# Token tiles of every fourth group of 32 tokens, and the gates' exchange moved around the rotary query products

## The chip, the cores and the metric

The kernel runs on one core of a Trainium2 chip. TensorE (PE) multiplies matrices into PSUM, ScalarE (ACT) and VectorE (DVE) work on PSUM and SBUF, GpSimd (POOL) and SyncE (SP) issue DMAs; the transfers of both queues run on the core's 16 DMA engines. The metric is the device time of one execution in microseconds, the median of several runs.

## The reference, cut to what matters

Two layers over 512 tokens of width 2048. Each layer normalises the tokens, projects them to 4928 columns, runs three groups of heads on the parts, gates the joined result, projects it back and adds it to the tokens:

```python
for l in range(DEPTH):                                  # 2
    z = rmsnorm(x, pre_norm_g[l]) @ w_in[l]             # (512, 2048) @ (2048, 4928)
    q_lat, kv_lat, k_pe, gb, gc, xin, q_mem, gate = split_cols(z)
    # group A: 8 heads; q and k carry 64 rotary columns beside 128 plain ones
    a_out = mla_attention(q, k, v)                      # softmax over all 512 positions, (512, 1024)
    # group B: width-3 convolution along the positions
    c_out = gb * conv3(gc * xin, conv_w[l])             # (512, 512)
    # group C: 4 heads over 256 memory tokens
    m_out = memory_attention(q_mem, rmsnorm(mem), ...)  # (512, 512)
    y = concatenate([a_out, c_out, m_out]) * silu(gate) # (512, 2048)
    x = x + rmsnorm(y @ w_o[l], post_norm_g[l])
```

The convolution is the one place where neighbouring positions meet; everything else treats a token alone or sums over all of them.

## The kernel before, in words

Tokens lie in four tiles of 128. Tile t holds the tokens 128 t to 128 t + 127, one to a partition, so a tensor "by tokens" is a slab [128 partitions, 4 tiles, 512 columns]. The two large projections (`group`, line 488) are done as a block scheme with seven products P1 to P7 in place of eight; every operand is split into two parts (`split_to`, line 275: ACT writes the rounded part, DVE the rest), and each product is three matmuls (`mm3`, lines 271 to 273).

A layer runs the input projection in five column groups, then the `mixer` (line 1248: four memory heads, then eight attention heads, with the query, key and value products of the next pair of heads between them), then the output projection (`out_proj`, line 1289).

Heads work "by features": y is kept as four slabs of [128 features, 4 blocks, 512 tokens]. The gate comes out of the projection by tokens and has to be turned. ACT applies SiLU (line 781), DVE turns every 32x32 block in place (`blocks_turned`, line 918, put off with `pr.defer` at the end of `gated`), and 16 DMAs on SP's queue put the blocks at their places (`exchange`, lines 922 to 929; a run is 32 numbers of 4 bytes). `gate_rows` (line 931) first calls `pr.until`, which issues put-off work until all four tiles are turned, then the 16 DMAs. This is done for three slabs in each layer: `gm` (beside the memory queries) during the last column group, `ga1` after the first plain query product of the mixer, `ga0` three steps further. The head's result is multiplied with the gate in place (line 1199). The convolution (`conv_turn`, line 937) transposes on PE, takes its three taps on DVE straight from PSUM, and multiplies with the transposed gb.

The rotary part of the queries (`q_rope_steps`, line 1034) is two products for four heads, and `rotate0`: four DVE products with the tables, a split, two DMAs away and, later, four DMAs back, all on POOL's queue.

After the heads, y is cut into quarters (`y_blocks`, line 1284; tokens 0 to 255 and 256 to 511) and split for the output projection. The last stage (`fin` and `residual`, lines 1325 and 1374) squares and sums the result, scales it, adds the old tokens (line 1382), and in the last layer sends each tile to the output from SP's queue, a row of the output from a partition (line 1384): two halves of 512 KB for each of the tiles 0 to 2, and five pieces for tile 3, 128, 128, 256, 256 and 256 KB.

Order: PE, SP and POOL issue in the order in which the program is written; ACT and DVE are ordered by a planner with a model of costs. Work given to `pr.defer` has a price and is issued where the steps' `room` allows it, or when `until` asks for it. Weights are loaded some eight units ahead through eight buffers, "raw", which the rotary tables and products share. SP takes its DMAs strictly in order, and the exchange stands between the weight loads.

```python
def exchange(dst, src):
    for p in range(4):
        for b in range(4):
            a = src[32 * p:32 * p + 32].rearrange("i t c k -> i (c t) k")[:, :, 32 * b:32 * b + 32]
            y = dst[32 * b:32 * b + 32].rearrange("i c (t k) -> i (c t) k", k=P)[:, :, 32 * p:32 * p + 32]
            nc.sync.dma_start(y, a)
```

Of the kernel before, what the change touches and what calls it, by code (L numbers as in the profile page):

```python
# [58 lines left out]
PI_DOWN = 3.1415925  # L59

RAW, PIECES, SLABS = 8, 4, 19


class Unit:
# [20 lines left out]
class Program:  # L85
# [23 lines left out]
    def add(self, fn, units=(), room=0.0, ahead=None):  # L109

        self.steps.append((list(units), fn, room, self.ahead if ahead is None else ahead))
# [115 lines left out]
def encoder(tc, x, xt, mem, memt, positions, columns, w_in, q_norm_g, w_uq, w_qr, kv_norm_g, w_ukv,  # L227
# [32 lines left out]
    def slab(name, dt=F32):  # L260
        return slabs.tile([P, D], dt, tag="slab", name=nm(name))

    def scrap(name, w=512, dt=F32):
        return piece.tile([P, 512], dt, tag="piece", name=nm(name))[:, :w]
# [135 lines left out]
    class Left:  # L400
# [1 line left out]

        def __init__(self, by_tokens):
            self.by_tokens = by_tokens
            self.ops = {}

        def split(self, name, p, src):
            t = self.ops[name, p] = slab(f"{name}{p}", F32R)  # L410
            c = src.shape[-1]
            split_to(t[:, :1024].rearrange("p (k c) -> p k c", c=c), t[:, 1024:].rearrange("p (k c) -> p k c", c=c), src)

# [3 lines left out]
        def stationary(self, name, kt, tt):  # L417
            if self.by_tokens:
                t, o = self.ops[name, tt], kt * P
            else:  # L420
                t, o = self.ops[name, kt // 4], (kt % 4) * 256 + tt * P
            return t[:, o:o + P], t[:, 1024 + o:1024 + o + P]

    def combine(left, p, a11, a12, a21, a22):
# [63 lines left out]
    def group(left, key, w, block, slot, passes, final, hold=None, by_two=False, direct=None):  # L488
# [51 lines left out]
        def ended(q, tt):  # L540
            ps = bk[q][tt][:, :w]
            s = {(i, j): slot(i, j, tt) for i in range(2) for j in range(2)}
            if len(s[0, 0].shape) == 3:
                ps = ps.rearrange("p (c k) -> p c k", c=4)
            if q == "P1":
                if keep:
                    nc.scalar.copy(s[1, 0], ps)
                    plus(s[0, 0], s[0, 0], ps)
                    final(0, 0, tt)
                elif apart:  # L550
                    nc.scalar.copy(s[1, 0], ps)
                elif passes is STEADY:
                    nc.scalar.copy(s[0, 0], ps)
                else:
                    plus(s[0, 0], s[0, 0], ps)
                    final(0, 0, tt)
            elif q == "P2":
                if shared:
                    nc.scalar.copy(s[0, 0], ps)
                else:  # L560
                    plus(s[0, 0], s[1, 0] if apart else s[0, 0], ps)
                    final(0, 0, tt)
            elif q == "P5":
                if apart:
                    plus(s[1, 1], s[1, 0], ps)
                else:
                    nc.scalar.copy(s[1, 0], ps)
            elif q == "P6":
                if apart:
                    plus(s[1, 1], s[1, 1], ps)  # L570
                else:
                    plus(s[0, 1], s[1, 0], ps)
            elif q == "P3":
                nc.vector.tensor_tensor(s[0, 1], ps, s[1, 1] if apart else s[0, 1], op=ALU.subtract)
                final(0, 1, tt)
            elif q == "P7":
                if apart:
                    nc.vector.scalar_tensor_tensor(s[1, 1], ps, -1.0, s[1, 1], op0=ALU.mult, op1=ALU.subtract)
                    plus(s[1, 0], s[1, 0], ps)
                else:  # L580
                    nc.scalar.copy(s[1, 1], ps)  # L581
                    nc.vector.scalar_tensor_tensor(s[1, 1], s[1, 1], -1.0, s[1, 0], op0=ALU.mult, op1=ALU.subtract)
                final(1, 1, tt)
            elif direct:
                direct(1, 0, tt, ps)
            else:
                if apart:
                    plus(s[1, 0], s[1, 0], ps)
                else:
                    nc.scalar.copy(s[1, 0], ps)  # L590
                final(1, 0, tt)
# [143 lines left out]
    def projection(l):  # L735
# [8 lines left out]
        def own(*names):  # L744
            def f():
                for n in names:
                    C[n] = slab(n).rearrange("p (c t k) -> p t c k", c=4, t=NT)
            return f

        def slot_of(a, b):  # L750
# [154 lines left out]
    def turn4(view, j, dst=None):  # L905

        ps = bank("tps")
        for t in range(NT):
            v = view(t)
            nc.tensor.transpose(ps[:, t * P:(t + 1) * P], v[:, j] if len(v.shape) == 3 else v[:, j * P:(j + 1) * P], G["ident"])  # L910
        return ps

    def y_slab(k):
        if k not in G["ys"]:
            G["ys"][k] = slab("y").rearrange("p (j c) -> p j c", j=4)
        return G["ys"][k]

    def blocks_turned(v):

# [2 lines left out]
    def exchange(dst, src):  # L922


        for p in range(4):
            for b in range(4):
                a = src[32 * p:32 * p + 32].rearrange("i t c k -> i (c t) k")[:, :, 32 * b:32 * b + 32]
                y = dst[32 * b:32 * b + 32].rearrange("i c (t k) -> i (c t) k", k=P)[:, :, 32 * p:32 * p + 32]
                nc.sync.dma_start(y, a)

    def gate_rows(k, name, C):
        def f():
# [3 lines left out]

    def conv_turn(l, c, C):
        def f():
            u = turn4(lambda t: C["gc"][:, t], c)
            y, w = y_slab(2)[:, c, :], G[f"cw{l}"]  # L940
            nc.vector.tensor_scalar_mul(y, u, w[:, 1, c:c + 1])
            nc.vector.scalar_tensor_tensor(y[:, 1:], u[:, :S - 1], w[:, 0, c:c + 1], y[:, 1:], op0=ALU.mult, op1=ALU.add)
            nc.vector.scalar_tensor_tensor(y[:, :S - 1], u[:, 1:], w[:, 2, c:c + 1], y[:, :S - 1],
                                           op0=ALU.mult, op1=ALU.add)
            g = turn4(lambda t: C["gb"][:, t], c)
            nc.vector.tensor_tensor(y, y, g, op=ALU.mult)
        return f

    def qm_turn(j, C):
# [187 lines left out]
    def head_iters(j, rope, src, keys, whole=False):  # L1137
# [50 lines left out]
        def av(b):  # L1188
            def g():
                if b == 0 or whole:  # L1190
                    st["o"] = bank("o")
                VH, VL = src()[1]
                o = st["o"] if whole else st["o"][:, b * 256:(b + 1) * 256]
                PT = st.pop("PT" if whole else ("PT", b))
                for k in range(kts):
                    mm3(o, (VH(k), VL(k)), (PT[0][:, k], PT[1][:, k]), k == 0, k == kts - 1)
                if b == 1:
                    y = G["ys"][j // 4][:, j % 4, :]
                    nc.vector.tensor_tensor(y, st["o"], y, op=ALU.mult)
            return g  # L1200
        return [((score(t), [], 0.4), trans(t), av(t // 2) if t == 3 or t == 1 and not whole else None, 4 if whole and kts > 2 else 5)
                for t in range(NT)]
# [45 lines left out]
    def mixer(l, C, pair2, tail):  # L1248
# [1 line left out]
        add(tables_fetch)  # L1250
        add(mem_fetch)
        (p0, rotate0, fetch0), (p1, rotate1, fetch1) = (q_rope_steps(l, g) for g in range(2))
        put(p0, rotate0)
        sts = [{} for _ in range(4)]
        qkv = qkv_steps(l, 0, sts[0])
        qkv[0] += (0.0, 1)
        qkv[2] += (0.0, 0)
        put(qkv[:1])
        add(gate_rows(1, "ga1", C))
        its = [it for i in range(4) for it in mem_head(i)]  # L1260
        m = len(its)
        between = {k: [s] for k, s in zip((2, 5, 8, 10, 12), qkv[1:])}
        between.setdefault(3, []).append((gate_rows(0, "ga0", C), []))
        between.setdefault(6, []).append((fetch0, []))
        between[m - 2] = [(lambda: pr.prep_next(), [])]
        for pair in range(4):
# [14 lines left out]
        pipeline(its, between, m)  # L1281


    def y_blocks(p):
        ys = G["ys"]
        a, b = ys[p], ys[2 + p]
        return a[:, :, :256], b[:, :, :256], a[:, :, 256:], b[:, :, 256:]

    def out_proj(l):
        last = l == depth - 1  # L1290
# [83 lines left out]
    def residual(l, st, t):  # L1374
# [4 lines left out]
        def part(c, n=1024):  # L1379
            cs = slice(c, c + n)  # L1380
            xt = st["x"][t]
            nc.vector.scalar_tensor_tensor(xt[:, cs], og[:, cs], st["r", t], xt[:, cs], op0=ALU.mult, op1=ALU.add)
            if last:
                nc.sync.dma_start(out[0][rows, cs], xt[:, cs])
            else:
                nc.gpsimd.dma_start(G["dst"][rows, cs], xt[:, cs])

# [35 lines left out]
    def put(*passes):  # L1423
        for steps in passes:
            for s in steps:
                add(*s)
# [20 lines left out]
    for l in range(depth):  # L1447
# [129 lines left out]
        lat = [latent_turn(l, "cq", j) for j in range(4)] + [latent_turn(l, "ckv", j) for j in range(2)] + [k_rope_turn]  # L1577
        more = [(f, []) for f in lat + [qm_turn(j, C) for j in range(4)]]
        put(weave(g4[16:], more, 2, 2))
        G["left"] = Y = Left(False)  # L1580
        g0, g1, gains, fetch = out_proj(l)

        def low(p):
            return lambda: G["left"].split("A12", p, G["ys"][2 + p][:, :, :256])

        def use_y(Y=Y):
            G["left"] = Y

        def sums(p):
            def f():  # L1590
                a, b = G["ys"][p], G["ys"][2 + p]
                left = G["left"]
                pr.defer(1.2, lambda: left.split("A11", p, a[:, :, :256]))
                pr.defer(1.2, lambda: left.split("A22", p, b[:, :, 256:]))
                combine(left, p, a[:, :, :256], b[:, :, :256], a[:, :, 256:], b[:, :, 256:])
            return f

        last_pair = {0: [(sums(0), []), g0[0][0]], 1: [g0[0][1]], 2: [g0[0][2]], 3: [g0[0][3]],
# [61 lines left out]
```

## Time and profile before

| | |
|---|---|
| median of three runs | 1475.88 us (1475.15 to 1478.01) |
| profiled execution: its own time | 1475.58 us |
| profiled execution: span, first to last instruction | 1473.8 us |
| TensorE busy | 1454.6 us |
| VectorE busy | 1102.1 us |
| ScalarE busy | 862.1 us |
| GpSimd busy | 269.9 us |
| mean granted TensorE clock | 0.998 |
| DMA packets in all | 193344, of them 60576 under 512 B |
| bytes moved | 295.21 MB |

The span is what the trace shows; the execution's own time is 1.8 us longer. Busy time says what an engine did, not what it held up; the tables of waits and the chain of work say that. "SPq" and "POOLq" are the queues that issue DMAs. "To landing" is the time from a DMA's issue until its data is there. A DMA share of 1.00 means that the packets of the transfers filled all 16 DMA engines.

### The profile page before, as it was taken

The page shows a single profiled execution, that of the slowest core. Times are in us where ns is not written, and L with a number is a line of the kernel's source. Part 1 is how long each engine was busy: PE and PEld are TensorE (multiplying, and loading weights), DVE is VectorE, ACT ScalarE, POOL GpSimd, SP SyncE. Part 2 cuts the span into 40 slices and gives each one's busy share as a digit, 9 for nine tenths or more (in the row PEclk, how much of TensorE's full clock was granted, in tenths as well). Part 3 has the DMA queues.
Part 4 walks back from the last instruction along what each step waited for, and adds up shares of the span by engine and source line. Part 5 has one row for each costly group of instructions (what it writes and reads, how often), then busy time and mean ns, then how long its engine had stood idle before and what let it go on. Part 6 is the DMA issues. An engine that isn't in the chain of part 4 may idle for free.

```text
span 1473.8 us, 19452 instructions
## 1 busy us (share of the span) xinstructions
PE 1454.6 (99%) x7104; PEld 1239.6 (84%) x7104; DVE 1102.1 (75%) x1469; ACT 862.1 (58%) x1312; POOL 269.9 (18%) x276
## 2 busy tenths in 40 slices
PE   9999999999999999999999999999999999999997
PEld 8887888899887888888898888888988878888886
DVE  5899677857577778868779666776576777788687
ACT  7856344446458788654777434444464686786443
POOL 0032302031301010321210333030322000004111
PEclk9999999999999999999999999999999999999999
DMA  9999978698989292695987999796979784128945
GB/s 358 403 274 219 219 188 179 166 195 221 207 232 165 75 275 91 124 231 154 339 289 227 235 232 223 195 170 173 210 199 214 230 157 104 40 86 153 266 110 186
DMA packets 193344, 295.21 MB, mean 200 GB/s; under 512 B 60576, under 2 KB 83616, under 8 KB 189408
## 3 DMA queue, kind: packets, MB, share of 16 engines
q0 software_dynamic: 56576, 129.51, 43.7%
q1 hardware_dynamic: 136672, 164.45, 36.3%
q8 instruction: 56, 0.92, 0.3%
q14 instruction: 40, 0.33, 0.1%
HBM read 266.01 MB, written 21.63 MB: 195 GB/s over the span
## 4 chain that ended last, share of the span: by engine, by line
PE 95%; DMA 2%; DVE 1%; ACT 1%; issue 0%; SPq 0%; POOLq 0%; DVEq 0%; ACTq 0%
PE P L272 23%; PE P L273 23%; PE P L271 23%; PE ptp L1184 2%; PE o L272 1%; PE o L273 1%; PE sc L273 1%; PE sc L271 1%; PE sc L272 1%; PE o L271 1%; PE tps L910 1%; PE sc L1165 1%; PE qps L272 1%; PE qps L271 1%; PE qps L273 1%; PE sc L1166 1%
## 5 line engine op out<-in xcount | busy, mean ns | idle before, releaser
L188 ACT CAST wh<-wr 128x1024 fp32r<-128x1024 f32 (+2 forms) x436 | 444.5, 1023 | 448.2 <-PE P L273 340.1
L189 DVE TENSOR_TENSOR wl<-wr,wh 128x1024 fp32r<-128x1024 f32 (+2 forms) x436 | 515.7, 1187 | 251.1 <-ACT wh L188 247.7
L271 PE MATMUL P<-wh,S 128*128 128x512 f32 (+1 forms) x896 | 345.3, 385 | 0.0
L273 PE MATMUL P<-wh,S 128*128 128x512 f32 (+1 forms) x896 | 343.9, 384 | 0.0
L272 PE MATMUL P<-wl,S 128*128 128x512 f32 (+1 forms) x896 | 343.9, 384 | 0.0
L272 PE MATMUL P<-wl,A 128*128 128x512 f32 (+1 forms) x656 | 252.2, 384 | 1.4 <-DVE wl L189 1.4
L271 PE MATMUL P<-wh,A 128*128 128x512 f32 (+1 forms) x656 | 253.1, 386 | 0.0
L273 PE MATMUL P<-wh,A 128*128 128x512 f32 (+1 forms) x656 | 251.9, 384 | 0.0
L145 POOL DMA_DIRECT2D wr<-in_w_in_dram x132 | 158.3, 1199 | 445.3 <-DVE wl L189 261.8
L273 PEld LDWEIGHTS P<-wh,S 128*128 128x128 f32 x896 | 168.3, 188 | 30.1
L272 PEld LDWEIGHTS P<-wl,S 128*128 128x128 f32 x896 | 168.4, 188 | 29.6
L271 PEld LDWEIGHTS P<-wh,S 128*128 128x128 f32 x896 | 168.3, 188 | 29.4
L272 PEld LDWEIGHTS P<-wl,A 128*128 128x128 f32 x656 | 123.3, 188 | 24.4 <-DVE wl L189 2.8
L273 PEld LDWEIGHTS P<-wh,A 128*128 128x128 f32 x656 | 123.2, 188 | 22.1
L271 PEld LDWEIGHTS P<-wh,A 128*128 128x128 f32 x656 | 123.2, 188 | 21.6 <-ACT og L581 0.2
L145 POOL DMA_DIRECT2D wr<-in_w_o_dram x40 | 48.4, 1248 | 297.8 <-DVE wl L189 294.1
L1171 ACT ACTIVATE P<-sc,nm 128x512 f32<-128x512 f32 (+1 forms) x96 | 59.2, 617 | 30.3 <-DVE nm L1168 29.7
L1168 DVE TENSOR_REDUCE nm<-sc 128x1 f32<-128x512 f32 (+1 forms) x96 | 56.9, 596 | 13.3 <-PE sc L273 7.1
L1174 ACT ACTIVATE P<-P,rec 128x512 f32<-128x512 f32 (+1 forms) x96 | 60.6, 652 | 6.6 <-DVE rec L1173 6.6
L1184 PE MATMUL ptp<-identr,P 128*128 128x128 f32 x320 | 46.5, 274 | 2.3 <-ACT P L1174 2.3
L1184 PEld LDWEIGHTS ptp<-identr,P 128*128 128x128 f32 x320 | 37.9, 141 | 9.5 <-ACT P L1174 2.7
L177 DVE TENSOR_TENSOR wr<-wr,wr 128x1024 f32<-128x1024 f32 (+1 forms) x36 | 42.2, 1175 | 3.6 <-DMA wr<-in_w_in_dram 3.2
(317 smaller groups left out, 2070.1 us busy)
## 6 DMA issues: line engine op xcount, KB each, us to landing
wr<-in_w_in_dram SPq DMA_DIRECT2D x128, 512.0 KB, 5.4
wr<-in_w_in_dram POOLq DMA_DIRECT2D x108, 512.0 KB, 7.6
wr<-in_w_o_dram SPq DMA_DIRECT2D x48, 512.0 KB, 6.4
wr<-in_w_o_dram POOLq DMA_DIRECT2D x40, 512.0 KB, 6.9
wr<-in_w_in_dram SPq DMA_DIRECT2D x32, 416.0 KB, 3.8
wr<-in_w_in_dram POOLq DMA_DIRECT2D x24, 416.0 KB, 6.0
wr<-in_w_mk_dram SPq DMA_DIRECT2D x15, 512.0 KB, 8.6
wr<-in_w_mv_dram SPq DMA_DIRECT2D x15, 512.0 KB, 10.5
```

The costliest lines, as they stand in the source:

```text
L145: engine.dma_start(dst, src, **kw)
L177: nc.vector.tensor_tensor(tiles[a], tiles[a], tiles[b], op=ALU.add)
L188: pin(nc.scalar.copy(hi[:, h], src[:, h]))
L189: pin(nc.vector.tensor_tensor(lo[:, h], src[:, h], hi[:, h].bitcast(F32), op=ALU.subtract))
L271: nc.tensor.matmul(ps, ah, bh, start=first, stop=False, **kw)
L272: nc.tensor.matmul(ps, ah, bl, start=False, stop=False, **kw)
L273: nc.tensor.matmul(ps, al, bh, start=False, stop=last, **kw)
L910: nc.tensor.transpose(ps[:, t * P:(t + 1) * P], v[:, j] if len(v.shape) == 3 else v[:, j * P:(j + 1) * P], G["ident"])
L1168: nc.vector.tensor_reduce(nmax, ps, axis=AX.X, op=ALU.max, negate=True)
L1171: nc.scalar.activation(pt, ps, AF.Exp, bias=nmax, accum_out=tot)
L1174: nc.scalar.activation(pt, pt, AF.Copy, scale=rec)
L1184: nc.tensor.transpose(ps[:, k * P:(k + 1) * P], pt[:, k * P:(k + 1) * P], G["ident"])
```

## The change

A tile now holds every fourth group of 32 tokens: partition 32 p + j of tile t is token 128 p + 32 t + j. The host hands over x and the positions in that order. The three gate slabs are laid out with the four tiles' blocks side by side, (group of 32 columns, tile, 32 columns), so that a run of the exchange is 128 numbers, 512 bytes, and y has its tokens in their natural order. What comes from PE by tiles (a transposed tensor, a head's result) is read through `of_tiles`, and y is read and written through `in_tiles`, both with runs of 32 numbers. The convolution needs neighbours, so ACT copies the transposed u to SBUF in natural order, ACT makes the middle tap, and DVE's two other taps read SBUF. The quarters of y for the output projection are taken with `y_half`, runs of 64 numbers, and `split` writes them in runs of 32 (`apart`). The output is written through a view that puts the tokens back: its first dimension is the four p, its second the 32 j. In the mixer, the exchange of `ga1` is issued ahead of the rotary products p0, the exchange of `ga0` between p0 and `rotate0`.

```diff
+BLOCKS = "gm", "ga0", "ga1"
         def split(self, name, p, src):
             t = self.ops[name, p] = slab(f"{name}{p}", F32R)
+            if self.apart:
+                hi, lo = (t[:, o:o + 1024].rearrange("p (t g j) -> p g t j", t=2, j=32) for o in (0, 1024))
+                split_to(hi, lo, src.rearrange("p g (t j) -> p g t j", j=32))
+                return
...
-                    C[n] = slab(n).rearrange("p (c t k) -> p t c k", c=4, t=NT)
+                    C[n] = slab(n).rearrange("p (g t j) -> p t g j" if n in BLOCKS else "p (t g j) -> p t g j", t=NT, j=32)
...
+    def of_tiles(a):
+        return a.rearrange("q (t p j) -> q t p j", t=NT, j=32)
+    def in_tiles(a):
+        return a.rearrange("q (p t j) -> q t p j", t=NT, j=32)
...
         for p in range(4):
             for b in range(4):
-                a = src[32 * p:32 * p + 32].rearrange("i t c k -> i (c t) k")[:, :, 32 * b:32 * b + 32]
-                y = dst[32 * b:32 * b + 32].rearrange("i c (t k) -> i (c t) k", k=P)[:, :, 32 * p:32 * p + 32]
-                nc.sync.dma_start(y, a)
+                a = src[32 * p:32 * p + 32].rearrange("i t (c b) j -> i c b (t j)", b=4)[:, :, b]
+                nc.sync.dma_start(dst[32 * b:32 * b + 32, :, P * p:P * p + P], a)
...
-            u = turn4(lambda t: C["gc"][:, t], c)
+            ps = turn4(lambda t: C["gc"][:, t], c)
             y, w = y_slab(2)[:, c, :], G[f"cw{l}"]
-            nc.vector.tensor_scalar_mul(y, u, w[:, 1, c:c + 1])
+            u = scrap("u")
+            nc.scalar.copy(in_tiles(u), of_tiles(ps))
+            nc.scalar.activation(y, u, AF.Copy, scale=w[:, 1, c:c + 1])
...
-            nc.vector.tensor_tensor(y, y, g, op=ALU.mult)
+            nc.vector.tensor_tensor(in_tiles(y), in_tiles(y), of_tiles(g), op=ALU.mult)
...
-                    nc.vector.tensor_tensor(y, st["o"], y, op=ALU.mult)
+                    nc.vector.tensor_tensor(in_tiles(y), of_tiles(st["o"]), in_tiles(y), op=ALU.mult)
...
-        put(p0, rotate0)
+        add(gate_rows(1, "ga1", C))
+        put(p0)
+        add(gate_rows(0, "ga0", C))
+        put(rotate0)
...
         put(qkv[:1])
-        add(gate_rows(1, "ga1", C))
...
-        between.setdefault(3, []).append((gate_rows(0, "ga0", C), []))
...
-    def y_blocks(p):
-        ys = G["ys"]
-        a, b = ys[p], ys[2 + p]
-        return a[:, :, :256], b[:, :, :256], a[:, :, 256:], b[:, :, 256:]
+    def y_half(k, h):
+        return G["ys"][k].rearrange("q c (p k) -> q (c p) k", k=P)[:, :, 64 * h:64 * h + 64]
...
             if last:
-                nc.sync.dma_start(out[0][rows, cs], xt[:, cs])
+                nc.sync.dma_start(out[0].rearrange("(p t j) c -> t p j c", t=NT, j=32)[t][:, :, cs], xt[:, cs])
...
+    def tiles(a):
+        return a.reshape(1, 4, NT, 32, -1).transpose(0, 2, 1, 3, 4).reshape(a.shape)
+    x, mem = tiles(np.asarray(inputs["x"])), np.asarray(inputs["mem"])
```

More of the change, by code (lines that the diff above doesn't have):

```diff
@@ L400, in encoder, with __init__ @@
     class Left:
-        def __init__(self, by_tokens):
-            self.by_tokens = by_tokens
+        def __init__(self, by_tokens, apart=False):
+            self.by_tokens, self.apart = by_tokens, apart
             self.ops = {}
@@ L420, in stationary @@
             else:
-                t, o = self.ops[name, kt // 4], (kt % 4) * 256 + tt * P
+                t, o = self.ops[name, kt // 4], (kt % 4) * P + tt * 512 if self.apart else (kt % 4) * 256 + tt * P
             return t[:, o:o + P], t[:, 1024 + o:1024 + o + P]
@@ L543, in ended @@
             if len(s[0, 0].shape) == 3:
-                ps = ps.rearrange("p (c k) -> p c k", c=4)
+                ps = ps.rearrange("p (g j) -> p g j", j=32)
             if q == "P1":
@@ L909, in turn4 @@
             v = view(t)
-            nc.tensor.transpose(ps[:, t * P:(t + 1) * P], v[:, j] if len(v.shape) == 3 else v[:, j * P:(j + 1) * P], G["ident"])
+            nc.tensor.transpose(ps[:, t * P:(t + 1) * P], v[:, 4 * j:4 * j + 4].rearrange("p g j -> p (g j)") if len(v.shape) == 3 else v[:, j * P:(j + 1) * P], G["ident"])
         return ps
@@ L1579, in encoder @@
         put(weave(g4[16:], more, 2, 2))
-        G["left"] = Y = Left(False)
+        G["left"] = Y = Left(False, True)
         g0, g1, gains, fetch = out_proj(l)
         def low(p):
-            return lambda: G["left"].split("A12", p, G["ys"][2 + p][:, :, :256])
+            return lambda: G["left"].split("A12", p, y_half(2 + p, 0))
         def use_y(Y=Y):
@@ L1590, in f @@
             def f():
-                a, b = G["ys"][p], G["ys"][2 + p]
+                a11, a12, a21, a22 = (y_half(k, h) for h in range(2) for k in (p, 2 + p))
                 left = G["left"]
-                pr.defer(1.2, lambda: left.split("A11", p, a[:, :, :256]))
-                pr.defer(1.2, lambda: left.split("A22", p, b[:, :, 256:]))
-                combine(left, p, a[:, :, :256], b[:, :, :256], a[:, :, 256:], b[:, :, 256:])
+                pr.defer(1.2, lambda: left.split("A11", p, a11))
+                pr.defer(1.2, lambda: left.split("A22", p, a22))
+                combine(left, p, a11, a12, a21, a22)
             return f
@@ L1640 @@
     nc = bacc.Bacc("TRN2", target_bir_lowering=False, num_devices=1, dynamic_dma_scratch_size=2048)
-    x, mem = np.asarray(inputs["x"]), np.asarray(inputs["mem"])
+    def tiles(a):
+        return a.reshape(1, 4, NT, 32, -1).transpose(0, 2, 1, 3, 4).reshape(a.shape)
+    x, mem = tiles(np.asarray(inputs["x"])), np.asarray(inputs["mem"])
     columns = np.concatenate([np.asarray(inputs[n]).reshape(-1, P) for n in ("pre_norm_g", "mem_norm_g", "conv_w")]).T
@@ L1644 @@
     given.update(
-        x=x, mem=mem, columns=columns, inv_freq=np.array(INV_FREQ, np.float32),
+        x=x, mem=mem, positions=tiles(given["positions"]), columns=columns, inv_freq=np.array(INV_FREQ, np.float32),
         xt=x[0].T.reshape(2, 8, P, 2, 256).transpose(3, 0, 2, 1, 4).reshape(2, 2, P, D),
```

## Prediction

> **What bounds the kernel now.** I read the page first, then TensorE's waits, then the chain of waits at the end, then the DMA views of the last 34 us.
>
> ```profile
> span 1473.8 us, 19452 instructions
> PE 1454.6 (99%) x7104; PEld 1239.6 (84%) x7104; DVE 1102.1 (75%) x1469; ACT 862.1 (58%) x1312; POOL 269.9 (18%) x276
> ...
> PE 95%; DMA 2%; DVE 1%; ACT 1%; issue 0%; SPq 0%; POOLq 0%; DVEq 0%; ACTq 0%
> ```
>
> TensorE is busy for all but 1473.8 - 1454.6 = 19.2 us, and the chain that ended last runs over it for 95%. The change takes no matmul away and adds none. So nothing that it does on ACT, DVE or a queue can win more than a share of 19.2 us; it can only lose, by making TensorE wait or by lengthening what comes before its first and after its last matmul. The waits in the middle (line waited on, us in total, times, longest):
>
> ```profile
> PE o L271 <- ACT PT L276: 3.7, 2, 1.9
> PE ptp L1184 <- ACT P L1174: 2.3, 2, 1.1
> ...
> PE o L272 <- DVE PT L277: 0.7, 2, 0.3
> ```
>
> They are 6.7 us, all in the first memory head of each layer, where the softmax goes from ACT to DVE and back. No row of that table names y, the gates' exchange or any DMA.
>
> The rest stands at the end. First the chain of waits there (start, length, what), then SP's queue, then the transfers from 1440 to 1474 us: GB/s in 40 slices of 0.85 us, the hardware queue's packets, MB and share of 16 engines' time, and the issues with KB each and us to landing.
>
> ```profile
> 1464.84 0.24 PE P L273
> 1465.16 0.60 ACT junk L1333
> ...
> 1467.71 1.99 DVE xr L1382 x3
> ```
> ```profile
> L1384 SPq DMA_DIRECT2D out_dram<-xr x11: 332/332/382, 1448.8 to 1469.7; - x11
> ```
> ```profile
> GB/s 207 277 414 434 231 19 0 0 0 0 39 135 154 366 308 361 390 96 366 251 0 19 289 419 405 121 0 0 77 419 405 333 0 237 293 376 306 22 0 10
> ...
> q1 hardware_dynamic: 1584, 4.20, 32.2%
> ...
> out_dram<-xr SPq DMA_DIRECT2D x6, 512.0 KB, 2.9
> ...
> out_dram<-xr SPq DMA_DIRECT2D x3, 256.0 KB, 2.6
> out_dram<-xr SPq DMA_DIRECT2D x2, 128.0 KB, 1.9
> ```
>
> TensorE ends at 1465.1, DVE's last piece at 1469.7, the eleventh write is issued at 1469.7 and lands some 2.6 us later, at 1472.3; the span ends 1.5 us after that. The slices with 0 GB/s between the writes show the point of it: each write is gone before the next is ready, so only the last one is seen in the time. This holds as long as a write runs at several hundred GB/s.
>
> **The output's view: the term that decides.** Before, a write's both sides begin with 128 rows. Now the DRAM side begins with 4 (p), then 32 (j), then the row. No transfer of the trace begins with so small a count: the loads, stores and rows begin with 128 partitions, the exchange and the rotary fetch with 32. So the trace does not show what such a write costs, and I bound it. One end is nothing: the same bytes in the same rows of 1 to 4 KB on 16 engines, 2.9 us for 512 KB. The other end is that the first dimension is what is dealt out to the engines, one p to each, so that 4 of 16 carry all of it. I take this end: all rows that fill 16 engines have a first count that 16 divides, and 4 leaves nothing for the other twelve. This is a reading of the pattern, and the one step that no row bears out.
>
> The Trainium skill, page "DMA: Bandwidth & Descriptors", section "Why a DMA increments its semaphore by 16 and not by 1", states it as a rule: the slowest dimension above 1 of both sides is looked at, and the largest engine count up to 16 that divides both is taken. By it, 4 and 128 give 4 engines; no run here shows it yet. Its weight would put the chance of this step still higher than I do.
>
> Price. The output is 512 x 2048 x 4 bytes = 4.19 MB, which is nearly all of the 4.20 MB in the q1 row. Slices that were full show 419 GB/s, 26.2 GB/s for an engine. Four engines move 105 GB/s: 4.19 MB take 40.0 us. The q1 row gives the slow end: 32.2% of 16 engines x 34 us = 175 engine-us, which is 43.8 us on four. The fastest slice, 434 GB/s, gives 38.7. I take 40.0, as a full slice is a saturated engine, while the packet times of the share also hold waiting beside other transfers.
>
> The writes then queue behind one another: a 512 KB piece takes 5.0 us, and the pieces of tiles 0 to 2 and the five of tile 3 are ready within 21 us. The queue never runs dry for long, so its end is the first issue, 1448.8, plus the part of a write that is not transfer, 1.9 - 128 KB / 419 GB/s = 1.6, plus 40.0: 1490.4. With the 1.5 us to the span's end, 1491.9, against 1473.8: **+18.1 us** (16.8 to 21.9 by the two other rates). TensorE's last wait, ACT's and DVE's tail are inside it and cost nothing more.
>
> The same page's table "Specifications" gives about 27 GiB/s for an engine; by that the 40.0 would be 36.2 and the sum +14.3 us. The full slices here are lower.
>
> **The exchange, shorter and earlier: 0.** First the tile y's rows (duration of an issue min/median/max, first and last start), then SP's queue and DVE around the mixer's start, then the rotary fetch and its first use.
>
> ```profile
> L929 SPq DMA_DIRECT2D y<-ga x64: 585/632/2558, 443.6 to 1200.3; - x64
> L929 SPq DMA_DIRECT2D y<-gm x32: 597/1796/4222, 379.9 to 1134.3; - x32
> ```
> ```profile
> 379.90 30.98 SPq L929 DMA_DIRECT2D y<-gm  x16
> ...
> 433.22 10.29 SPq L145 DMA_DIRECT2D wr<-in_memt_dram  x2
> ```
> ```profile
> 443.56 28.61 SPq L929 DMA_DIRECT2D y<-ga  x32
> 472.35 1.04 SPq L145 DMA_DIRECT2D wr<-in_w_uq_dram  x2
> ```
> ```profile
> 423.44 0.71 DVE L920 STREAM_TRANSPOSE ga<-ga 128x512 f32<-128x512 f32 x1 [0.29 <-ACT ga L781]
> ```
> ```profile
> 434.24 0.72 DVE L920 STREAM_TRANSPOSE ga<-ga 128x512 f32<-128x512 f32 x1 [0.42 <-ACT ga L781]
> ...
> 436.98 1.22 DVE L1053 TENSOR_TENSOR rm<-qr,tab 128x1024 f32<-128x1024 f32 x1
> ```
> ```profile
> 450.64 1.08 POOL L1076 DMA_DIRECT2D QR<-qrd  x2 [1.22 <-DMA qrd<-rm]
> ```
> ```profile
> 470.54 0.23 PE sc L1165
> ```
>
> An exchange DMA has 32 partitions x 16 runs = 512 packets of 128 B; it becomes 128 of 512 B. Over 96 DMAs 49152 packets become 12288. SP's 31 us for the 16 DMAs of gm and 28.6 us for the 32 of ga shrink, and the engines get room. But no wait of TensorE ends on any of this, so the gain is 0. The move: 32 DMAs go from after 443.6 to about 424 (ga1, its tiles being turned) and 435.0 (ga0). The new wait is SP's for the last turn at 434.96, and behind it stand two loads of the memory tokens, which waited until 443 in any case, and the query weights now issued at 472.4, which come earlier. DVE has turned ga0 before the rotary product of 436.98 already, so `until` brings nothing forward. POOL's rotary fetch, issued by 451.7 and needed at 470.5, keeps over 10 us and meets less traffic. Were this cover gone, the price is the stall that TensorE has there now.
>
> What can move beside it is the planner's order of ACT and DVE in the first memory head. I put it at 0, between -6.7 (the stalls go) and +6.7 (they double).
>
> **The convolution: 0.** L941 leaves DVE, ACT gets two passes over 512 numbers, priced by its copies from PSUM. The window rows give TensorE, loads, DVE, ACT, POOL busy.
>
> ```profile
> L941 DVE TENSOR_SCALAR y<-tps,cols x8: 708/750/751, 224.7 to 975.8; 128x512 f32<-128x512 f32 x8
> ```
> ```profile
> L567 ACT COPY gm<-P x4: 587/587/587, 239.1 to 971.5; 128x512 f32<-128x512 f32 x4
> ```
> ```profile
> 222.00:259.00 37.00, 37.00 (x181) 31.03 (x180) 27.96 (x33) 15.51 (x17) 11.85 (x10) 1.00 0.88 176
> ...
> 555.00:592.00 37.00, 37.00 (x184) 30.89 (x183) 33.22 (x49) 30.24 (x54) 0.00 (x0) 1.00 0.28 86
> ```
>
> Per layer ACT gains 4 x 2 x 0.59 = 4.7 us and DVE loses 4 x 0.75 = 3.0 us, in a stage where ACT is idle for 21 us of 37 and TensorE for none. The tap is one step longer, but only y waits for it, and y's slab is read again only after the heads. If ACT were full there, it would cost up to 4.7 us a layer.
>
> **Finer runs: 0.** Splits and sums of y, 1024 numbers, now go in runs of 32 and 64. The rows: a split of y with runs of 256, and a copy of 512 numbers with runs of 32.
>
> ```profile
> L276 ACT CAST S<-y x16: 1033/1049/1056, 567.4 to 1356.8; 128x1024 fp32r<-128x1024 f32 x16
> L277 DVE TENSOR_TENSOR S<-y,S x16: 1206/1218/1226, 569.0 to 1357.9; 128x1024 fp32r<-128x1024 f32 x16
> ```
> ```profile
> L385 DVE COPY widecos<-cos x1: 427/427/427, 296.5 to 296.5; 128x512 f32<-128x512 f32 x1
> ```
>
> The copy runs at 0.83 ns a number, no slower than the split's 1.19, so I leave the durations as they are. At the costly end, the in-place turn's 0.70 us for 512 (434.24 above), a pass of DVE takes 1.4 in place of 1.22: 22 of them a layer add 4 us, against 3.8 us of idle DVE in the fullest window (555 to 592) alone. At most some 2 us a layer would reach TensorE.
>
> **Sum.** 1475.58 + 18.1 = 1493.7, say 1494; the median of the runs lies 0.3 us above the profiled execution.
>
> **The rivals.**
> A. The writes keep 16 engines, whatever the view (same rows, same bytes). Then everything else is covered: 1475.6. For it: 512 KB in 2.9 us now, and rows that do not change. Against it: the first count of 4.
> B. The writes keep 16 engines and the freed queue, or another order on ACT, ends the first memory head's stalls: 1475.6 - 6.7 = 1468.9, so faster by 0.5%. It decides once a probability tile is ready 1.9 us sooner. For it: the exchange fills the DMA engines during that head. Against it: the stalls end on ACT and DVE, never on a DMA. A stall cut by half gives 1472.2, just past the limit.
> C. 16 engines, and the stalls double, by y's slabs being claimed earlier and SP standing for a free one: 1482.3. It decides when the weights of 472.4 come later than now. Against it: SP reaches them about 10 us sooner if nothing stops it.
>
> **How the numbers follow.** A measurement of this kernel tells 0.2%, 2.95 us, from no change. Forecast 0.80, A 0.10, B 0.06, C 0.04. So faster 0.06 (B), same 0.10 (A), slower 0.84 (forecast and C). The forecast's own range: 16.8 to 21.9 by the rates, widened by the 6.7 us of stalls that may go and a few that may come, and by an engine alone being quicker than one among sixteen: 1484 to 1500. It leaves out A, B and C, together 0.20.
>
> **What would show it.** In the changed profile the issue-to-landing time of the 512 KB output writes should be over 5 us for the first and rise from write to write, to 15 us or more for the later ones; the GB/s of the last 40 us should stand near 105 without slices of 0, and the DMA share near a quarter; TensorE should still end near 1465. Packets under 512 B should fall by 49152, and SP's stretch of y<-gm from 31 us to well under half. If the 512 KB writes still land in about 3 us, the deciding step is wrong, and the time is A's or B's. If they spread over four engines but the time is below 1484, an engine is faster than the full slices show.

## The result and the profile after

The changed kernel takes 1496.95 us (median of 4 runs, 1496.37 to 1497.34), the kernel before, timed beside it, 1476.24 us. The ratio is 1.0139, 95% interval 1.0121 to 1.0156: the change costs 1.4%. The forecast was 1494, with 1484 to 1500 as its range.

First the head of the changed kernel's page, with the chain's shares by engine; then TensorE's waits.

```profile
span 1494.5 us, 19452 instructions
PE 1453.4 (97%) x7104; PEld 1239.8 (83%) x7104; DVE 1096.8 (73%) x1461; ACT 871.7 (58%) x1328; POOL 270.0 (18%) x276
...
DMA packets 156348, 295.21 MB, mean 198 GB/s; under 512 B 11292, under 2 KB 46620, under 8 KB 152412
...
PE 94%; DMA 2%; ACT 1%; DVE 1%; SPq 0%; issue 0%; POOLq 0%; DVEq 0%; ACTq 0%
```
```profile
PE kps L272 <- ACT P L1185: 4.2, 2, 2.3
...
PE ptp L1198 <- ACT P L1188: 0.8, 2, 0.5
PE sc L272 <- ACT P L1185: 0.6, 2, 0.3
```

TensorE's busy time is 1.2 us less than before and its waits in the middle are 5.6 us in place of 6.7. So the 20.7 us that the span grew are not in the middle at all. The chain of waits, the output's row and the transfers from 1440 us on (same columns as before the change, slices of 1.4 us) show where they are.

```profile
1461.92 0.24 PE P L274
...
1462.24 0.60 ACT junk L1346
...
1464.79 1.99 DVE xr L1395 x3
```
```profile
L1397 SPq DMA_DIRECT2D out_dram<-xr x11: 536/822/4854, 1445.9 to 1479.6; - x11
```
```profile
DMA  6000488222232222222222222222221222222100
GB/s 268 0 0 0 60 328 357 86 107 107 101 119 104 104 107 104 104 107 104 107 104 104 104 107 107 104 104 104 74 70 46 96 104 103 101 101 103 70 7 6
...
q1 hardware_dynamic: 1452, 4.19, 19.6%
```

TensorE ends at 1462.2, 2.9 us earlier than before, and DVE's last piece at 1466.8. Then 25 us follow in which nothing but the output is moving. The slices stand at 104 GB/s with a DMA share of two tenths, where before there were bursts of up to 419 and zeros between them. SP is held up as well: an issue takes up to 4.9 us, and the last one goes out at 1479.6, 12.8 us after DVE has finished the data. For the issues on SP's queue this trace gives no time to landing.

### The profile page after: what moved, and what is told of

It is laid out like the page before. It is cut to its first block, busy times and chain, and to the rows that moved or that the text cites. A ratio compares the mean times of both kernels' runs of the same rounds, so it can differ in the third digit from the quotient of the medians.

```text
span 1494.5 us, 19452 instructions
## 1 busy us (share of the span) xinstructions
PE 1453.4 (97%) x7104; PEld 1239.8 (83%) x7104; DVE 1096.8 (73%) x1461; ACT 871.7 (58%) x1328; POOL 270.0 (18%) x276
## 4 chain that ended last, share of the span: by engine, by line
PE 94%; DMA 2%; ACT 1%; DVE 1%; SPq 0%; issue 0%; POOLq 0%; DVEq 0%; ACTq 0%
PE P L272 23%; PE P L273 23%; PE P L274 23%; PE ptp L1198 2%; PE o L273 1%; PE o L272 1%; PE o L274 1%; PE sc L274 1%; PE sc L272 1%; PE sc L273 1%; PE tps L915 1%; PE sc L1179 1%; PE qps L272 1%; PE qps L274 1%; PE qps L273 1%; PE sc L1180 1%
## 5 line engine op out<-in xcount | busy, mean ns | idle before, releaser
L273 PEld LDWEIGHTS P<-wl,A 128*128 128x128 f32 x656 | 123.2, 188 | 23.4 <-DVE wl L190 1.9
```

What stands on the lines that cost most here:

```text
L273: nc.tensor.matmul(ps, ah, bl, start=False, stop=False, **kw)
```

## The experiments

Theory: the output's view begins with 4, and the first count decides how many of the 16 DMA engines carry a write. Rival 1: rows of the output that lie in scattered groups of 32 are slow to write, whatever engine carries them. Rival 2: the loss comes from another part of the change.

### Four writes of 32 rows in place of one that begins with 4

```diff
-                nc.sync.dma_start(out[0].rearrange("(p t j) c -> t p j c", t=NT, j=32)[t][:, :, cs], xt[:, cs])
+                for p in range(4):
+                    nc.sync.dma_start(out[0, P * p + 32 * t:P * p + 32 * t + 32, cs], xt[32 * p:32 * p + 32, cs])
```

> The changed kernel with one edit: every write of the output is cut into four, one for each p, so that both sides begin with 32 rows; all four are issued by SP. Theory (the first count of the view decides how many engines carry a write): the writes land in about 2 us again, nothing queues; TensorE ends near 1462 as in the changed kernel. The last tile has 20 issues of 0.33 us in place of 5, which SP works off from 1464.4 to 1471; with 1.8 us to land and 1.5 us to the end the span is about 1474 and the time 1475 to 1477. Rival 1 (rows of the output that lie in scattered groups of 32 are slow to write): still 1490 or more. Rival 2 (the loss is elsewhere in the change): still about 1497.

Measured: 1478.35 us, ratio to the kernel before 1.0008 (0.9999 to 1.0017). The 1.4% are gone, with the same rows going to the same scattered places. Rivals 1 and 2 fall as causes of the loss. The output's row, and the issues from 1440 us on:

```profile
L1398 SPq DMA_DIRECT2D out_dram<-xr x44: 314/420/1321, 1445.1 to 1472.7; - x44
```
```profile
out_dram<-xr SPq DMA_DIRECT2D x24, 128.0 KB, 2.4
...
out_dram<-xr SPq DMA_DIRECT2D x12, 64.0 KB, 1.7
out_dram<-xr SPq DMA_DIRECT2D x8, 32.0 KB, 1.6
```

The writes land in 1.6 to 2.4 us. The expected 1475 to 1477 were missed by a little: an issue took 0.42 us at the median, not 0.33, and SP was still issuing at 1472.7.

### Half of the last tile's issues on ACT

```diff
-                    nc.sync.dma_start(out[0, P * p + 32 * t:P * p + 32 * t + 32, cs], xt[32 * p:32 * p + 32, cs])
+                    (nc.scalar if t == NT - 1 and p % 2 else nc.sync).dma_start(
+                        out[0, P * p + 32 * t:P * p + 32 * t + 32, cs], xt[32 * p:32 * p + 32, cs])
```

> As the kernel that cuts every write into four, but for the last tile two of the four are issued by ACT, which is idle by then. Theory: the last tile's issues take 3.3 us on each queue and follow DVE's pieces; DVE ends at about 1466.8, the last write lands near 1469.5, span about 1471, time 1472 to 1474, 0.15 to 0.25% below the kernel before. Rival 1 and rival 2: 1490 or more.

Measured: 1481.24 us, ratio 1.0032 (1.0023 to 1.0041). Better than the changed kernel, but slower than with SP alone, against the expectation. The output's rows, and SP's waits from 1440 us on:

```profile
L1398 SPq DMA_DIRECT2D out_dram<-xr x34: 314/410/1468, 1447.2 to 1478.0; - x34
L1398 ACTq DMA_DIRECT2D out_dram<-xr x10: 377/434/523, 1465.7 to 1470.2; - x10
```
```profile
SPq L1398 <- DMA out_dram<-xr: 9.1, 5, 7.1
```

ACT issued its ten by 1470.2 as expected, but SP now waited 9.1 us for writes to the output to land, a wait that its queue did not have when it issued them all. Two queues that write one tensor got a wait between them. Why the program holds it was not tried, and the wait is not shown to be the whole of the 2.9 us: in this profile TensorE also ended later, at 1463.4 against 1461.4 with SP alone.

### The view alone, and a view as scattered that begins with 16 or 8

On the kernel before, with j = 32 (first count 4), j = 8 (first count 16) and j = 16 (first count 8):

```diff
-                nc.sync.dma_start(out[0][rows, cs], xt[:, cs])
+                nc.sync.dma_start(out[0].rearrange("(p t j) c -> t p j c", t=NT, j=32)[t][:, :, cs], xt[:, cs])
```

> The kernel before with one edit: the output is written through the view that begins with 4 (p), then 32 (j); nothing else is changed, so the tokens come out in another order. Theory: four engines, 105 GB/s; the changed kernel took 48.6 us from its first write (1445.9) to the end of the span (1494.5), so 1448.8 + 48.6 = 1497.4 and a time of 1497 to 1500. Rival 1 (scattered groups of 32 rows): the same. Rival 2 (the loss is elsewhere): 1476.

Measured: 1501.02 us, ratio 1.0161 (1.0147 to 1.0175). The one line costs the whole loss and a little more, 1 us over the expected range. From the first write, 1450.8, to the end of the span, 1499.3, it took 48.5 us, as expected; the first write came 2.0 us later than the 1448.8 of the sum, as TensorE ended later in this execution (1467.1 against 1465.1).

> The kernel before with one edit: the output is written through a view that begins with 16 groups of 8 rows, four times as scattered as the change's 4 groups of 32; the tokens come out in another order. Theory: 16 divides by 16, all engines carry the write, no change: 1475 to 1477, with the 512 KB writes landing in about 3 us. Rival 1 (scattered groups are slow): as slow as the view that begins with 4 or slower, 1495 or more.

Measured: 1477.58 us, ratio 1.0005 (0.9995 to 1.0015): no change in the time, though its rows lie in groups of 8. This is the sharpest of the runs: the same line with another count, 16 in place of 4, and rows more scattered for it.

> The kernel before with one edit: the output is written through a view that begins with 8 groups of 16 rows; the tokens come out in another order. Theory (the largest count up to 16 that divides the first count): 8 engines, 210 GB/s. A 512 KB write takes 2.5 us and no longer piles up, only the last tile's 1 MB does: it takes some 5 to 6 us from 1468.7, so the span grows by 2 to 4 us and the time is 1478 to 1481. If every count under 16 fell to one fixed small number of engines, it would be 1495 or more; if only the count 4 were bad, 1476 to 1477.

Measured: 1484.51 us, ratio 1.0047 (1.0029 to 1.0065). Between the two, as the theory has it, but by 8 us where 2 to 4 were expected. The transfers from 1440 us on of the three views, in this order: first count 4, 8, 16, in slices of 1.5, 1.1 and 1.5 us, with the row of the output's queue.

```profile
GB/s 82 195 367 371 33 0 0 93 344 262 98 104 106 117 101 109 104 104 106 106 104 106 104 107 106 101 109 104 101 82 66 60 100 100 104 102 104 81 10 5
...
q1 hardware_dynamic: 1452, 4.19, 17.9%
```
```profile
DMA  6999940000589554545554455545455555541000
GB/s 71 169 191 362 422 182 0 0 0 0 102 342 350 208 208 186 102 98 171 168 98 138 167 204 204 153 113 171 197 191 165 153 181 182 204 168 53 0 7 0
...
q1 hardware_dynamic: 1496, 4.19, 28.2%
```
```profile
GB/s 318 421 82 0 0 44 218 289 352 145 167 194 106 251 235 107 158 333 266 191 315 134 5 0 0 0 0 0 0 0 0 0 0 0 0 0 0 0 0 0
...
q1 hardware_dynamic: 1584, 4.20, 23.4%
...
out_dram<-xr SPq DMA_DIRECT2D x6, 512.0 KB, 4.0
```

Four engines hold 104, eight reach 204 at a share of five tenths, sixteen go to 333 (the slice of 352 holds loads too). The packet counts tell the engines apart without a rate. The eleven writes have 1408 rows, and the queue has 176 packets more before the change and with 16, which is 11 x 16; with 4 it has 44 more, 11 x 4, and with 8 it has 88, 11 x 8. In the traces these are packets of 4 bytes, and one for each engine that a write uses fits all four kernels.

Eight do not hold their 204: slices of 98 to 171 stand between. The estimate took the full rate throughout, and the writes did pile up. The engines were not idle in those slices, as the share stays at four or five tenths; the packets took longer. In engine-us (engines times the microseconds that they were busy) the queue's packets took 17.9% of 16 x 60 us = 172 with 4, about as the 175 before the change, but 28.2% of 16 x 45 = 203 with 8 and 23.4% of 16 x 60 = 225 with 16. So eight engines that are never idle need 25.4 us for the output, not the 20 of the full rate. What makes the packets longer was not separated.

### The move of the exchange without the new layout, and the layout without the move

On the kernel before, the mixer's lines of the change alone (`gate_rows` of `ga1` ahead of p0, of `ga0` behind it):

```diff
-        put(p0, rotate0)
+        add(gate_rows(1, "ga1", C))
+        put(p0)
+        add(gate_rows(0, "ga0", C))
+        put(rotate0)
...
-        add(gate_rows(1, "ga1", C))
...
-        between.setdefault(3, []).append((gate_rows(0, "ga0", C), []))
```

> The kernel before with one edit: the exchange of ga1 issued ahead of the rotary products and that of ga0 behind them, as in the change; layout, runs of 128 B and output as before. In the changed kernel TensorE ended 2.9 us earlier than before and DVE took the rotary products at 445.8 in place of 437.0, after the first softmax work. Theory M (the move alone brings this, through the planner's order of ACT and DVE): stalls in the first memory heads as in the changed kernel, TensorE's end near 1462, time 1473 to 1474. Theory L (the shorter exchange brings it): stalls as before, 1475.5 to 1477. A third case: runs of 128 B issued there fill SP and the engines for some 30 us while the rotary products and the memory tokens' loads want them, and the time rises to 1478 or more.

Measured: 1480.34 us, ratio 1.0022 (1.0013 to 1.0031): slower. TensorE's waits, and DVE's rotary products around 448:

```profile
PE sc L271 <- DVE rm L1063: 3.7, 2, 1.8
PE sc L271 <- DVE PT L277: 1.9, 2, 1.1
...
PE kps L271 <- ACT P L1171: 1.3, 2, 0.6
```
```profile
447.97 1.20 DVE L1053 TENSOR_TENSOR rm<-qr,tab 128x1024 f32<-128x1024 f32 x1
```

DVE takes the rotary products 11 us later than before (436.98), behind the first softmax work and in one stretch with the splits, and the score products wait for it. So the move does change the planner's order, but this order is no better: the waits named are 3.7 + 1.9 + 1.3 us and more, against 6.7 before. The third case of the expectation gave the right time for another reason than the one it named: the waits end on DVE, not on a transfer.

The other way round, the mended kernel (writes of 32 rows) with the exchange at its old place:

```diff
-        add(gate_rows(1, "ga1", C))
-        put(p0)
-        add(gate_rows(0, "ga0", C))
-        put(rotate0)
+        put(p0, rotate0)
...
+        add(gate_rows(1, "ga1", C))
...
+        between.setdefault(3, []).append((gate_rows(0, "ga0", C), []))
```

> The changed kernel with every write of the output cut into four, and with the exchange issued where it was before the change (ga1 after the first plain query product, ga0 three steps on). The twin with the moved exchange took 1478.4. Theory M: the first memory heads stall as before the change, so 1479 to 1481. Theory L: as the twin, 1477.5 to 1479.

Measured: 1480.71 us, ratio 1.0029 (1.0018 to 1.0040), with the stalls of before:

```profile
PE o L272 <- ACT PT L277: 3.7, 2, 1.9
PE ptp L1198 <- ACT P L1188: 2.3, 2, 1.1
...
PE o L273 <- DVE PT L278: 0.7, 2, 0.3
```

So neither the move nor the layout removes them; the order in which ACT and DVE take the softmax changes for the better only where both are there.

### Fewer issues at the end

The mended kernel, the last tile as two halves:

```diff
-        if last and t == NT - 1:
-            pr.defer(0.4, lambda: part(0, 256))
-            pr.defer(0.4, lambda: part(256, 256))
-            pr.defer(0.7, lambda: part(512, 512))
-            pr.defer(0.7, lambda: part(1536, 512))
-            pr.defer(0.7, lambda: part(1024, 512))
-        else:
-            pr.defer(1.2, lambda: part(0))
-            pr.defer(1.2, lambda: part(1024))
+        pr.defer(1.2, lambda: part(0))
+        pr.defer(1.2, lambda: part(1024))
```

> The changed kernel with every write of the output cut into four (32 rows on both sides), all on SP, and the last tile sent as two halves of 1024 columns in place of five pieces: 8 issues in place of 20. In the twin with five pieces SP issued until 1473 while DVE had ended at 1466. If the issues were what kept the end, SP now issues the last at about 1467.5, it lands some 2.2 us later, and the span ends near 1471.3: 1473 to 1474.5, 0.15 to 0.25% below the kernel before. If not, 1477 to 1479 as the twin.

Measured: 1474.67 us, ratio 0.9988 (0.9979 to 0.9997), just over the expected range. This is faster than the kernel before and, by 1.5%, than the changed one. To see what in it does this, it was timed again on one chip beside its twin with the exchange at the old place and beside the kernel before with the same two halves (the edits are those shown above).

> The twin once more, on the same chip as the kernel with the exchange at its old place: 0.998 to 1.000 of the kernel before, as in its first runs.

Measured: 1473.81 us, ratio 0.9982 (0.9974 to 0.9990).

> The changed kernel with writes of 32 rows, the last tile sent as two halves, and the exchange issued where it was before the change. Its twin with the moved exchange took 0.9988 of the kernel before. If the move, together with the runs of 512 B, brings TensorE's earlier end, this one has the stalls of before (6.7 us in the first memory heads against 5.5) and takes 1476 to 1478, 0.1 to 0.2% above the twin. If the move brings nothing, the two agree within 0.1%.

Measured: 1476.85 us, ratio 1.0001 (0.9993 to 1.0010).

> The kernel before with one edit: the last tile is sent as two halves of 1024 columns in place of five pieces, 128 rows each. If the halves alone made the gain of the kernel that has them, this is 0.1 to 0.2% faster than the kernel before. If the gain is TensorE's, this is the same or up to 1 us slower: DVE's last piece begins later and is larger, and 5 issues of 0.33 us were no limit.

Measured: 1475.38 us, ratio 0.9992 (0.9983 to 1.0001).

The first memory heads in the three, in this order: mended with halves, old place of the exchange, kernel before with halves.

```profile
PE kps L272 <- ACT P L1185: 4.2, 2, 2.3
PE ptp L1198 <- ACT P L1188: 1.5, 2, 1.0
```
```profile
PE o L272 <- ACT PT L277: 3.7, 2, 1.9
PE ptp L1198 <- ACT P L1188: 2.3, 2, 1.1
```
```profile
PE o L271 <- ACT PT L276: 3.7, 2, 1.9
PE ptp L1184 <- ACT P L1174: 2.3, 2, 1.1
```

Halves alone are not told apart from no change. Layout and halves without the move: no change either. With the move: 0.18% faster. So the move is worth some 3 us, but only with the new layout; with the old one it costs 0.22%.

TensorE's progress shows where the 3 us lie. These are its first turned rotary keys and its first products with the fetched rotary queries in layer 1, with the memory heads between them, first without the move and then with it:

```profile
L1021 PE MATMUL krps<-identr,krA x4: 223/240/251, 420.3 to 420.6; 128*128 128x128 f32 x4
L1179 PE MATMUL sc<-KAB,QR x13: 389/393/397, 471.6 to 519.3; 128*128 128x512 f32 x13
```
```profile
L1021 PE MATMUL krps<-identr,krA x4: 223/240/251, 418.2 to 418.4; 128*128 128x128 f32 x4
L1179 PE MATMUL sc<-KAB,QR x14: 389/391/397, 467.7 to 518.0; 128*128 128x512 f32 x14
```

From the start of the one to the start of the other it is 51.3 us without the move and 49.5 with it, in layer 2 as well: 1.8 us a layer. In the five profiles that have both the layout and the move the stretch takes 49.3 to 50.2 us, in the two with the layout alone 51.3 to 51.5, with the move alone 52.0 and 52.7. With neither it takes 51.1 to 51.5 eight times out of ten and 49.9 or 50.0 twice. The waits named in the tables differ by less, 4.2 + 1.5 + 0.6 = 6.3 us against 6.7, so those tables alone do not show the gain. That the shorter runs on the queue are what let the planner choose the better order was not tried by itself, so it stays open which of the layout's edits does it.

## Why the prediction was right, point by point

**The output's view.** The step that no row bore out is now shown: one changed line gives the loss (first count 4), the same line with first count 16 gives none, 8 lies between, and four writes of 32 rows take it away. The rule on the page "DMA: Bandwidth & Descriptors" of the Trainium skill, section "Why a DMA increments its semaphore by 16 and not by 1", agrees: 104, 204 and up to 333 GB/s for 4, 8 and 16 engines, and a share of two and five tenths for the first two. The 27 GiB/s for an engine in the same page's table "Specifications", which is 29.0 GB/s, is higher than the 104 / 4 = 26.0 GB/s that these writes held.

**Its price.** The sum had 18.1 us; the span grew by 20.7, and that is a sum of misses of both signs: the first write came 2.9 us earlier, the transfers took 4.8 us longer, and the end of the span lay 2.2 us behind them in place of 1.5. That the total is off by only 2.6 us is in part luck. Issue to end of transfer was put at 1.6 + 40.0 us from the first write. It was 46.4, from 1445.9 to about 1492.3, read from stretches of the changed kernel (columns: stretch; busy us of TensorE, its loads, DVE, ACT, POOL; clock, DMA share, GB/s):

```profile
1472.00:1476.00 4.00, 0.00 (x0) 0.00 (x0) 0.00 (x0) 0.00 (x0) 0.00 (x0) 0.50 0.26 105
...
1480.00:1482.00 2.00, 0.00 (x0) 0.00 (x0) 0.00 (x0) 0.00 (x0) 0.00 (x0) 0.50 0.24 61
1484.00:1488.00 4.00, 0.00 (x0) 0.00 (x0) 0.00 (x0) 0.00 (x0) 0.00 (x0) 0.50 0.26 102
```

The rate for rows of 4 KB is the one forecast, 105. In the middle of the last tile's two small pieces, whose rows have 1 KB, it is 61, and the rows of 2 KB go at 102, terms that the sum did not have. At the start, from 1448 to 1452, only 0.20 MB of the output moved while the last load of old tokens, 0.62 MB in the same four microseconds, held the engines (39.9% of their time, the output 12.2%). The choice between the two rates was the wrong way round: the packets' time in q1 before the change, 175 engine-us, divided by four gives 43.8, nearer to the measured 44.8 than the 40.0 of full slices. That row already held the small rows and the waiting beside other transfers, which I took for a reason to set it aside. In the changed kernel q1's 19.6% of 16 engines x 54.5 us is 171 engine-us: the work of the engines hardly changed in this kernel, only their number.

**The exchange.** That it is off TensorE's path held: no wait of TensorE in the changed kernel names y or a transfer. Packets under 512 B fell by 49284 where 49152 were worked out; the other 132 are the 176 - 44 small packets of the output's writes. SP's stretch for gm fell from 31 to 19 us, not to well under half, and the 32 DMAs of ga did not get shorter at all: 18.0 + 12.1 us against 28.6. These are the changed kernel's stretches, first gm's, then ga's and the query weights behind them:

```profile
378.85 19.24 SPq L941 DMA_DIRECT2D y<-gm  x16
...
426.49 17.97 SPq L941 DMA_DIRECT2D y<-ga  x16
...
446.36 12.08 SPq L941 DMA_DIRECT2D y<-ga  x16
...
459.21 0.93 SPq L146 DMA_DIRECT2D wr<-in_w_uq_dram  x2
```

The query weights did come 13 us earlier, and a load of the memory tokens moved between the two exchanges. The exchange of ga0 went out at 446.4 and not at the 435.0 of the prediction, as SP stood at ga1's until 444.5. The rotary fetch had 9.5 us from its last issue to its use, where it had 18.8 before; TensorE still did not wait for it.

That DVE has turned ga0 before the rotary product already, so that `until` brings nothing forward, held: the last turn came at 433.17, at the same place in DVE's order as before. The term that was wrong is the planner's order, put at 0. It did change: the rotary products went from 436.98 to 445.75 on DVE, behind the first softmax work.

```profile
433.17 0.71 DVE L933 STREAM_TRANSPOSE ga<-ga 128x512 f32<-128x512 f32 x1 [0.43 <-ACT ga L786]
...
445.75 1.21 DVE L1067 TENSOR_TENSOR rm<-qr,tab 128x1024 f32<-128x1024 f32 x1
```

With it TensorE's waits in that place went from 6.7 to 5.6 us and its end came 2.9 us earlier, inside the bound of 6.7 that was kept for the range. Of the 2.9 us, 2.2 lie in the stretch of the memory heads (49.4 and 49.9 us in the two layers, 50.0 and 51.5 before); the rest is no more than what executions with the old order and layout differ by, whose TensorE ended at 1464.6 to 1467.4 in five profiles. Where no tail covers it, the gain is there to be timed, but it is the pair of layout and move that has it.

**The convolution and the finer runs.** No wait of TensorE names either, as worked out. The middle tap on ACT takes 727 ns where I priced 590 by a copy, and the two DVE taps from SBUF are no quicker than those from PSUM (750 and 751 ns against 743 and 751). The splits in runs of 32 take what those in runs of 256 took:

```profile
L277 ACT CAST S<-y x16: 1038/1052/1057, 565.8 to 1353.9; 128x1024 fp32r<-128x1024 f32 x16
L278 DVE TENSOR_TENSOR S<-y,S x16: 1208/1218/1226, 567.4 to 1355.0; 128x1024 fp32r<-128x1024 f32 x16
...
L955 ACT ACTIVATE y<-u,cols x8: 713/727/727, 225.7 to 974.7; 128x512 f32<-128x512 f32 x8
L956 DVE SCALAR_TENSOR_TENSOR y<-u,cols,y x8: 715/750/750, 226.4 to 976.0; 128x511 f32<-128x511 f32 x8
```

**The signs named in advance.** GB/s near 105 without zeros and a share near a quarter came out; TensorE ended at 1462.2, not near 1465; the rising time to landing can't be read, as the trace gives none for that queue; the waiting shows in SP's issues instead.

## What to carry to other kernels

Look at the first count of both sides of every DMA that a new layout touches: 4 in place of 128 left a quarter of the engines to the write, and it showed in the time because no work covered it at the end. Splitting such a write into ones whose first count is a multiple of 16 mends it, at the price of more issues, so send fewer and larger pieces with it. Price a transfer on fewer engines by the engine time that its packets took before, divided by the new count, not by the best rate. That can still be short: it was near for 4 engines (43.8 us for 44.8), but short for 8 (21.9 us for 25.4), where the packets themselves took longer.

## What the runs showed that was not expected

- The view that begins with 16 costs at the issue and in the transfer, though it has all 16 engines and the kernel's time is the same: SP's issue took 560 ns at the median in place of 332, and a 512 KB write landed in 4.0 us in place of 2.9 (against the kernel before). Whether the further dimension or the rows in groups of 8 do this was not separated.
- On four engines the issues themselves back up: up to 4.9 us for one, so SP is held long after the data is ready.
- Rows of 1 KB went at 61 GB/s on four engines where rows of 4 KB went at 105.
- Sharing the last writes between SP and ACT cost 0.24% against SP alone (1.0032 to 1.0008); SP then waited 9.1 us for writes to the same tensor.
